# Moving columns in short runs: the value products of a hybrid encoder layer read and write in another order

## The chip, the cores and the metric

The kernel runs on one core of a Trainium2 chip. A core has a matmul engine (TensorE, "PE" in the profile, its weight loads "PEld"), VectorE (DVE), ScalarE (ACT), GpSimd (POOL) and SyncE (SP), which issues most of the transfers. Operands lie in on-chip memory of 128 partitions; products add up in another memory of 128 partitions, whose banks hold 512 numbers of four bytes per partition. The metric is the device time of one execution in microseconds, the median of several runs, lower is better.

## The reference

One layer of an encoder trunk on 256 tokens of width 2048, all in fp32: a norm, one wide projection, an attention branch with latent vectors, a state-space branch run forward and backward, two gates, an output projection, and a gated feed-forward block with a short convolution. The change lies in the attention branch, in the values `v`:

```python
kv = (rms_norm(kv_lat, kv_norm_w) @ w_ukv).reshape(bsz, s_len, MLA_HEADS, QK_NOPE_DIM + V_HEAD_DIM)
k_nope, v = kv[..., :QK_NOPE_DIM], kv[..., QK_NOPE_DIM:]
...
p = jax.nn.softmax(sc.astype(jnp.float32) * scale, axis=-1).astype(v.dtype)
return jnp.einsum("bhqk,bkhd->bqhd", p, v)
```

`kv_lat` has 512 channels, `v` has 16 heads of 128 channels, so the values are a product of 256 x 512 by 512 x 2048.

## The kernel before

All products are made from two halves of each fp32 number. A value is rounded to the matmul engine's fp32r format (the high part) and the rest is kept (the low part); a product is then three: high by high, high by low, low by high. For a matmul, the stationary operand (`lhsT`, 128 x 128) is loaded first, and the moving operand (`rhs`, 128 partitions by up to 512 columns) streams past it; each of its columns adds into the column of the sums that stands at the same place in the output's order.

The work is a list of *jobs*. A job loads one slab of weights (128 partitions x 16 blocks of 128 columns) into one of three `raw` buffers, splits it in two halves of 8 blocks (`split_to`: ScalarE makes `wh` at L215, VectorE makes `wl` at L216, five buffers of each), and runs its products. Splits run up to five halves ahead of the products and loads up to three slabs ahead. Evacuations and small work ("sides") are attached to places in the list. The opening of the kernel is put in order by hand; after it, a planner orders the instructions of each engine by their place in the list and its own costs, with waits where buffers or results are needed.

The list of this stage has gate jobs (`g`: L277 to L279), rope jobs (`R`), value jobs (`V`) and query-key jobs (`QK`: L221 to L223), written out by hand at L1495:

```python
for it in "g R0 g g g V0 QK0 g QK1 g V1 QK2 g QK3 V2 R1 g QK4 g QK5 g V3 QK6 g QK7 g g g g g".split():
```

A value job (`v_job`, one for each group of four heads) has the latent tokens as its stationary operand (`hi` and `lo`, four blocks of 128 channels by 256 tokens) and the slab as its moving one. A half of the slab holds two blocks of channels, each with 512 value columns side by side. For each half `h`, token block `t` and channel block `kk` it makes three products of 512 columns (L663, L664, L665) into a bank of sums; the two token blocks have a bank each. So a job has 2 x 2 x 2 x 3 = 24 products, and the four jobs have 96. At the end, ScalarE copies the sums' high part (L670) and VectorE takes the rest (L671); attention multiplies them later (`att3`, L221 to L223 with `vh` and `vl`).

Elsewhere in the kernel, the dense products (L242) have a moving operand of two runs of 256 columns, the high and the low part of a page of tokens, and write 512 contiguous sums; L249 follows them with 256 contiguous columns.

Of the kernel before, what the change touches and what calls it, by code (L numbers as in the profile page):

```python
# [65 lines left out]
def tile_bidir_hybrid_layer(ctx: ExitStack, tc, xT, pos, vec, cst, w_in, w_r, w_v, w_qk, w_oa,  # L66
# [9 lines left out]
    act, dve, pe = nc.scalar, nc.vector, nc.tensor  # L76

    def page(shape, dt=F32, name="pg"):
        return pp.tile(shape, dt, tag="pg", bufs=NPG, name=name)
# [4 lines left out]
    def gpsum(shape):  # L84
        return gps.tile(shape, F32, tag="g", name="g")
# [4 lines left out]
    def f32(ap):  # L90
        return ap.bitcast(F32)
# [523 lines left out]
    def r_job(i):  # L615
# [30 lines left out]
        jobs.append(j)  # L646
        return j, ro

    def v_job(i):
        hi, lo = lat["kvHL"]  # L650
        cell = {}

        def mm(h, n, wh, wl):
            if h == 0:
                cell["ps"] = [gpsum([P, 512]), gpsum([P, 512])]
            wH = wh.rearrange("p (k b) m -> p k (b m)", k=2)
            wL = wl.rearrange("p (k b) m -> p k (b m)", k=2)
            for t in range(2):
                ts = slice(t * P, (t + 1) * P)
                for kk in range(2):  # L660
                    k = 2 * h + kk
                    ps = cell["ps"][t]
                    pe.matmul(ps, lhsT=hi[:, k, ts], rhs=wH[:, kk, :], start=k == 0, stop=False)  # L663
                    pe.matmul(ps, lhsT=hi[:, k, ts], rhs=wL[:, kk, :], start=False, stop=False)  # L664
                    pe.matmul(ps, lhsT=lo[:, k, ts], rhs=wH[:, kk, :], start=False, stop=k == 3)  # L665

        def ev():
            vh, vl = page([P, 2, 512], F32R, name="vh"), page([P, 2, 512], F32R, name="vl")
            for t in range(2):
                act.activation(vh[:, t, :], cell["ps"][t], AF.Copy)  # L670
                dve.tensor_sub(vl[:, t, :], cell["ps"][t], f32(vh[:, t, :]))  # L671
            vv[i] = (vh, vl)
        j = Job(w_v[i], 16, mm, ev)
        jobs.append(j)
        return j
# [808 lines left out]
    def Vj(i):  # L1484
        defer(v_job, w_v, i)
# [28 lines left out]
    for g in range(G):  # L1514
        b = len(jobs)
# [22 lines left out]
    b = len(jobs)  # L1538
# [23 lines left out]
    b = len(jobs)  # L1562
# [12 lines left out]
    b = len(jobs)  # L1575
# [134 lines left out]
    while i < len(jobs):  # L1710
# [3 lines left out]
        if j.whole:  # L1714
            ps = j.whole()
# [106 lines left out]
```

## Time and profile before

| | us |
|---|---|
| median of 3 runs | 1931.13 (1930.81 to 1931.7) |
| profiled execution | 1931.8 |
| its span | 1930.0 |
| TensorE busy | 1918.2 |
| VectorE busy | 1609.9 |
| ScalarE busy | 1284.1 |
| first and last start of a value product (L663) | 94.5 and 213.1 |

The profile is of one execution. Its span runs from the first to the last instruction; the execution's time has 1.8 us more around it. A row of a group gives line, engine, operation, output and inputs, shapes and count, then busy time, mean length of one in ns, and the idle time before. A matmul's length includes the time that its last columns take to come out, so lengths of successive matmuls overlap, and the pace is read from their starts in the timeline.

### The profile page before, as it was taken

The numbers are of one execution on the slowest core, as the hardware profiler recorded it, in microseconds if no ns is written. First come the engines' busy times: TensorE is split into PE (matmuls) and PEld (weight loads), VectorE is DVE, ScalarE is ACT, GpSimd is POOL, SyncE is SP. The second block draws the span as 40 slices with busy tenths as digits, with TensorE's granted clock in tenths as the row PEclk, the third lists the DMA queues.
The fourth block names the chain that finished last, engine by engine and source line by source line (L and its number), as shares of the span: only waits on it lengthen the run. The fifth ranks groups of instructions, "written<-read, shape, count | busy, mean of one in ns | idle before, by whom it ended". The sixth has DMA issues, their size and how long they took to land.

```text
span 1930.0 us, 28942 instructions
## 1 busy us (share of the span) xinstructions
PE 1918.2 (99%) x10834; PEld 1675.3 (87%) x10834; DVE 1609.9 (83%) x2628; ACT 1284.1 (67%) x2038; POOL 17.3 (1%) x38
## 2 busy tenths in 40 slices
PE   9999999999999999999999999999999999999998
PEld 8899988888888888888888888888888888888887
DVE  7887779979779779779898886898989889898675
ACT  6566555878887888878665555776656566655564
POOL 0200000000000000000000000000000000000000
PEclk9999999999999999999999999999999999999999
DMA  8644447765665565564566675567766666668983
GB/s 298 197 166 142 162 134 233 269 228 168 216 233 170 209 239 169 204 240 164 173 197 201 214 270 200 202 224 227 250 238 230 215 221 224 217 219 326 312 308 118
DMA packets 180525, 416.15 MB, mean 216 GB/s; under 512 B 11392, under 2 KB 114496, under 8 KB 152480
## 3 DMA queue, kind: packets, MB, share of 16 engines
q1 hardware_dynamic: 178816, 412.06, 63.3%
q0 software_dynamic: 1088, 1.67, 0.3%
q8 instruction: 85, 1.39, 0.3%
q10 hardware_dynamic: 480, 0.57, 0.1%
q14 instruction: 56, 0.46, 0.1%
HBM read 398.29 MB, written 13.34 MB: 213 GB/s over the span
## 4 chain that ended last, share of the span: by engine, by line
PE 92%; DVE 3%; DMA 2%; ACT 1%; issue 0%; SPq 0%; DVEq 0%; ACTq 0%
PE g L242 37%; PE g L249 19%; PE g L985 9%; PE s L1178 5%; PE g L277 3%; PE g L278 3%; PE g L279 3%; PE s L985 2%; DVE wl L216 1%; PE g L221 1%; DMA raw<-in_w_os 1%; PE g L223 1%; PE g L222 1%; PE s L242 1%; PE s L890 1%; PE s L899 1%
## 5 line engine op out<-in xcount | busy, mean ns | idle before, releaser
L216 DVE TENSOR_TENSOR wl<-raw,wh 128x1024 fp32r<-128x1024 f32 x621 | 745.6, 1214 | 183.2 <-ACT wh L215 104.6
L215 ACT ACTIVATE wh<-raw 128x1024 fp32r<-128x1024 f32 x621 | 641.4, 1049 | 274.9 <-PE g L242 89.6
L242 PE MATMUL g<-xHL,wh 128*128 128x512 f32 x1408 | 337.7, 392 | 0.3 <-DVE cu L292 0.3
L242 PE MATMUL g<-hHL,wh 128*128 128x512 f32 x1408 | 327.4, 390 | 0.0
L242 PEld LDWEIGHTS g<-hHL,wh 128*128 128x128 f32 x1408 | 262.6, 188 | 53.8 <-ACT wh L215 0.3
L242 PEld LDWEIGHTS g<-xHL,wh 128*128 128x128 f32 x1408 | 259.6, 188 | 52.0 <-PE s L223 0.4
L249 PEld LDWEIGHTS g<-xHL,wl 128*128 128x128 f32 x1408 | 180.5, 191 | 6.8
L249 PE MATMUL g<-xHL,wl 128*128 128x256 f32 x1408 | 182.6, 283 | 0.0
L249 PEld LDWEIGHTS g<-hHL,wl 128*128 128x128 f32 x1408 | 174.8, 192 | 3.4
L249 PE MATMUL g<-hHL,wl 128*128 128x256 f32 x1408 | 176.0, 283 | 0.0
L985 PE MATMUL g<-wh,yHL 128*128 128x512 f32 x392 | 124.9, 390 | 0.0
L152 ACT ACTIVATE wh<-T 128x1024 fp32r<-128x1024 f32 x60 | 63.6, 1061 | 58.6 <-DVE T L191 22.9
L277 PE MATMUL g<-wh,xHL 128*128 128x512 f32 x256 | 100.4, 392 | 0.0
L278 PE MATMUL g<-wl,xHL 128*128 128x512 f32 x256 | 100.0, 390 | 0.0
L279 PE MATMUL g<-wh,xHL 128*128 128x512 f32 x256 | 99.8, 390 | 0.0
L1123 DVE SCALAR_TENSOR_TENSOR uc<-u,V,uc 128x255 f32<-128x255 f32 x176 | 84.5, 480 | 15.3 <-ACT uc L1121 14.1
L153 DVE TENSOR_TENSOR wl<-T,wh 128x1024 fp32r<-128x1024 f32 x60 | 73.4, 1223 | 16.4 <-ACT wh L152 14.1
L985 PEld LDWEIGHTS g<-wh,yHL 128*128 128x128 f32 x392 | 73.6, 188 | 15.2
L242 PE MATMUL g<-aHL,wh 128*128 128x512 f32 x336 | 79.8, 390 | 0.0
L985 PE MATMUL g<-wl,yHL 128*128 128x512 f32 x196 | 76.5, 390 | 0.9 <-DVE wl L216 0.9
L1121 ACT ACTIVATE uc<-u,V 128x256 f32<-128x256 f32 x88 | 52.3, 595 | 34.4 <-DVE u L292 31.1
L242 PEld LDWEIGHTS g<-aHL,wh 128*128 128x128 f32 x336 | 62.6, 188 | 12.7
(413 smaller groups left out, 3078.1 us busy)
## 6 DMA issues: line engine op xcount, KB each, us to landing
raw<-in_w_in SPq DMA_DIRECT2D x88, 1024.0 KB, 4.8
raw<-in_w_up SPq DMA_DIRECT2D x88, 1024.0 KB, 4.8
raw<-in_w_in SPq DMA_DIRECT2D x128, 256.0 KB, 4.0
raw<-in_w_os SPq DMA_DIRECT2D x32, 1024.0 KB, 6.2
raw<-in_w_dn SPq DMA_DIRECT2D x44, 512.0 KB, 4.7
raw<-in_w_dn SPq DMA_DIRECT2D x66, 256.0 KB, 4.9
raw<-in_w_oa SPq DMA_DIRECT2D x16, 1024.0 KB, 5.7
FB<-acsD SPq DMA_DIRECT2D x32, 512.0 KB, 7.3
```

What stands on the lines that cost most here:

```text
L152: act.activation(wh, v, AF.Copy)
L153: dve.tensor_sub(wl, v, f32(wh))
L215: act.activation(vh, r, AF.Copy)
L216: dve.tensor_sub(vl, r, f32(vh))
L242: pe.matmul(ps, lhsT=wh[:, b, :], rhs=x, start=k == 0, stop=False)
L249: pe.matmul(cell["ps"][:, 0, :], lhsT=wl[:, b, :], rhs=get(k)[:, 0, :], start=False, stop=k == ktot - 1)
L277: pe.matmul(ps, lhsT=x[:, 0, ts], rhs=wH[:, kk, :], start=k == 0, stop=False)
L278: pe.matmul(ps, lhsT=x[:, 0, ts], rhs=wL[:, kk, :], start=False, stop=False)
L279: pe.matmul(ps, lhsT=x[:, 1, ts], rhs=wH[:, kk, :], start=False, stop=k == kt - 1)
L985: pe.matmul(M[nm], lhsT=x, rhs=w, start=left[nm] == total[nm], stop=left[nm] == 1)
L1123: dve.scalar_tensor_tensor(o[:, a], u[:, b], vcol("fcw", k * 88 + cb), o[:, a], ALU.mult, ALU.add)
L1178: pe.matmul(M[nm], lhsT=x, rhs=w, start=left[nm] == 3 * NK, stop=left[nm] == 1)
```

## The change

The products at L663 and L664 walk their moving columns and their sums in another order. A view of 512 columns is seen as four places of 128 columns. With `w = 16` the walk takes 16 columns of the first place, 16 of the second, of the third and of the fourth, then the next 16 of the first, and so on; with `w = 2` it takes two of each in turn. The high-by-high product goes in runs of 16, the high-by-low product in runs of 2; the low-by-high product (L665 before) keeps its contiguous order. The moving operand and the sums are viewed in the same way, so each column still adds into the same sum. Stationary operands, loads, splits and evacuations are the same.

```diff
+    def in_runs(ap, w):
+        return ap.rearrange("p (b m w) -> p m b w", b=4, w=w)
+
     def v_job(i):
...
-                    pe.matmul(ps, lhsT=hi[:, k, ts], rhs=wH[:, kk, :], start=k == 0, stop=False)
-                    pe.matmul(ps, lhsT=hi[:, k, ts], rhs=wL[:, kk, :], start=False, stop=False)
+                    pe.matmul(in_runs(ps, 16), lhsT=hi[:, k, ts], rhs=in_runs(wH[:, kk, :], 16), start=k == 0,
+                              stop=False)
+                    pe.matmul(in_runs(ps, 2), lhsT=hi[:, k, ts], rhs=in_runs(wL[:, kk, :], 2), start=False,
+                              stop=False)
                     pe.matmul(ps, lhsT=lo[:, k, ts], rhs=wH[:, kk, :], start=False, stop=k == 3)
```

## The prediction

> **What bounds the kernel now.** I read the totals of the page and the clock line first, then the chain that ended last, then the waits of TensorE from the first value job to the end.
>
> ```profile
> span 1930.0 us, 28942 instructions
> PE 1918.2 (99%) x10834; PEld 1675.3 (87%) x10834; DVE 1609.9 (83%) x2628; ACT 1284.1 (67%) x2038; POOL 17.3 (1%) x38
> PEclk9999999999999999999999999999999999999999
> PE 92%; DVE 3%; DMA 2%; ACT 1%; issue 0%; SPq 0%; DVEq 0%; ACTq 0%
> ...
> PE g L985 <- DVE wl L216: 0.9, 2, 0.5
> PE s L1276 <- ACT m L1256: 0.7, 1, 0.7
> PE g L242 <- DVE cu L292: 0.3, 1, 0.3
> PE s L1178 <- DVE wl L153: 0.2, 1, 0.2
> ```
>
> The matmul engine is busy for 99% of the span at full granted clock and makes up 92% of the chain. From 94 us on (the first value job starts at 94.53) it waits for 0.9 + 0.7 + 0.3 + 0.2 = 2.1 us in all. So a product that holds the array longer moves the end by nearly the same amount: at most 2.1 us can be swallowed by later waits. Busy time alone wouldn't prove this, because a matmul's record includes its drain; that is why the starts are read next.
>
> The three lines of the value job, and the first and last rows of the first job (V0) and the last (V3), from the timeline (start, length, instruction):
>
> ```profile
> L663 PE MATMUL g<-wh,latH 128*128 128x512 f32 x32 | 12.6, 393 | 0.0
> L664 PE MATMUL g<-wl,latH 128*128 128x512 f32 x32 | 12.5, 391 | 0.0
> L665 PE MATMUL g<-wh,latL 128*128 128x512 f32 x32 | 12.5, 390 | 0.0
> L664 PEld LDWEIGHTS g<-wl,latH 128*128 128x128 f32 x32 | 6.0, 188 | 1.1
> ...
> 94.53 0.39 PE L663 MATMUL g<-wh,latH 128*128 128x512 f32 x1
> 94.76 0.39 PE L664 MATMUL g<-wl,latH 128*128 128x512 f32 x1
> ...
> 99.75 0.39 PE L665 MATMUL g<-wh,latL 128*128 128x512 f32 x1
> 99.97 0.28 PE L221 MATMUL g<-latH,wh 128*128 128x256 f32 x1
> ...
> 208.32 0.40 PE L663 MATMUL g<-wh,latH 128*128 128x512 f32 x1
> ...
> 213.56 0.39 PE L665 MATMUL g<-wh,latL 128*128 128x512 f32 x1
> 213.79 0.28 PE L221 MATMUL s<-pT,vh 128*128 128x256 f32 x1
> ```
>
> V0 has 24 products between 94.53 and 99.97: 5.44 / 24 = 226.7 ns from start to start. V3 has 24 in 213.79 - 208.32 = 5.47, or 227.9 ns. The 390 ns in the group rows is the length of one product with its drain; the pace is 227 ns, and the pace is what counts. A weight load takes 188 ns, inside that pace. No row shows an idle gap before any of the 96 products. All four jobs together hold the array for 96 x 0.227 = 21.8 us, 1.1% of the span. The two changed lines are 64 of these products, 14.5 us.
>
> **How much of the pace is columns.** Products of 256 columns run beside products of 512:
>
> ```profile
> 396.92 3.79 PE L242 MATMUL g<-xHL,wh 128*128 128x512 f32 x16
> 400.55 2.08 PE L249 MATMUL g<-xHL,wl 128*128 128x256 f32 x16
> 402.46 3.82 PE L242 MATMUL g<-xHL,wh 128*128 128x512 f32 x16
> ```
>
> The sixteen of 256 columns take 402.46 - 400.55 = 1.91 us, 119.4 ns each. Against 226.7 ns for 512, a column costs (226.7 - 119.4) / 256 = 0.419 ns, so 512 columns cost 214.6 ns and 12.1 ns are fixed.
>
> **The change, part by part.** Nothing is added or removed: the same 10834 matmuls, the same weight loads (the stationary operand is untouched), the same loads from memory, the same waits. Both operands that take the new order take the same one, so that column 5 of the slab still adds into column 5 of the sums. What changes is the walk. With runs of 16 (L663), a product reads 32 runs and jumps 31 times. With runs of 2 (L664), it reads 256 runs and jumps 255 times. Each jump goes 128 columns, or 512 bytes, further along, and after the fourth place back. Reads of the slab and writes of the sums make it together.
>
> *The jump itself.* The trace of before has no product with runs this short. The nearest rows are those of L242: its moving operand is two runs of 256 columns (the high and the low part of a token page), one jump per product, while its sums lie contiguous. Sixteen of them take 400.55 - 396.92 = 3.63 us, 226.9 ns each, against 226.7 ns for the contiguous V0. A jump on the read side therefore costs 0.2 ns, with a resolution of some 0.9 ns (0.01 us on each sum, over 16 and 24 products). The bound below is nothing. The bound above is 0.2 + 0.9 = 1.1 ns a jump; there are 32 x (31 + 255) = 9152 jumps, 10.1 us. I take nothing, since the rows of one jump and none agree to 0.2 ns, and keep both ends.
>
> *A read or write that uses only part of what it fetches.* This isn't priced by the jump of L242, whose runs are long. If pairs are too short for the array's rate, the plainest price is half rate, one more 214.6 ns per product: 32 x 0.2146 = 6.87 us for the pairs alone, 13.7 us if runs of 16 suffer as well. I take nothing here too, nearest to the row that has any jump at all.
>
> The Trainium skill speaks on both sides. Advanced Engine Details and Errata (SBUF Cachelines) has lines of 16 bytes and asks for two hits in a line to keep full performance: a pair of fp32 is exactly two. Its next section (PSUM Cachelines) has lines of 8 bytes and asks that every two consecutive elements be contiguous, which a pair meets, and yet says that any non-contiguous access pattern slows matmuls significantly. By the first two statements the sum stays at +0; by the last all 64 products lose, and the rival "both kinds" below is what that would be here. No run here has yet shown any of it.
>
> *Adding to a sum written shortly before.* With one order throughout, a column of the sums is written again 512 columns later. With the orders in turn the distance shrinks: column 127 is the 506th of the order in pairs and the 128th of the contiguous product behind it, so 134 columns or 56 ns lie between. From an L665 to an L663 on the same bank (16 of the 32; the others follow on the other bank) the least is 176 columns. The rows of L249 show sums written again after 256 columns at the full pace (119.4 ns), and no row shows less. Bound below: nothing. Bound above, if 256 columns were needed: (256 - 134) x 0.419 = 51 ns for each of 32 L665, and (256 - 176) x 0.419 = 34 ns for 16 of the L663, 1.6 + 0.5 = 2.1 us. I take nothing; even the whole of it would lie within what can be told from no change.
>
> *Covers.* The edit is costed at nothing because the columns stream at the same rate, not because something hides it; there is no cover, as the waits show. If a product grew, what is late next is in the waits and the groups around these jobs (85 to 240 us):
>
> ```profile
> ACT vh L670 <- PE g L665: 2.1, 4, 0.8
> ACT wh L215 <- PE g L279: 17.2, 11, 2.5
> ...
> L670 ACT ACTIVATE vh<-g 128x512 fp32r<-128x512 f32 x8 | 4.7, 597 | 2.1 <-PE g L665 2.1
> ```
>
> ScalarE reads the finished sums (L670), and it already waits for them and for free slab buffers (L215, 17.2 us in these rows); it would wait a bit longer and then be no later relative to TensorE, since it and VectorE are ahead here. They gain room.
>
> *A gain.* A product can't stream fewer than its 512 columns; if all of the fixed 12.1 ns vanished from 64 products, that would be 0.8 us. Together with every later wait (2.1) it is 2.9 us, under 0.2%.
>
> The sum: the profiled execution took 1931.8 us, its span 1930.0 and 1.8 around it; plus 0 it stays 1931.8. That execution lies 0.7 above the median of the three runs, 1931.13 (1930.81 to 1931.7). The forecast is stated against that median: **1931.1 us, no change**. A measurement of this kernel tells about 0.2%, 3.9 us, from no change.
>
> **The rivals.**
>
> *Pairs at half rate (the other side: slower).* One mechanism: in L664, reading or writing pairs from four places fetches more than it uses, so that the 512 columns take twice as long; runs of 16 are long enough. +6.87 us, 1938.0. It decides as soon as a pair costs more than 3.9 / 32 = 122 ns extra per product, 57% above its columns' time. For it: no product before has runs under 128 columns, so nothing shows that pairs stream. Against it: a jump alone is free to 0.2 ns.
>
> *A fixed price per jump.* One column (0.419 ns) lost at each of 9152 jumps: 3.83 us, 1935.0, right at the bound. The L242 rows allow it (1.1 ns) but point lower.
>
> *Both kinds at half rate.* 13.7 us, 1944.9. It would need runs of 16, 64 bytes long, to be as bad as pairs; against it stands the same L242 row, though for reads only.
>
> *Dearer pairs.* A quarter of the rate, 3 x 214.6 x 32 = 20.6 us, 1951.7; nothing in the trace speaks for it.
>
> *The walk isn't what changes.* If the order of instructions moves (from the 94.53 us of V0 on, a planner fills in the work of several jobs), the time goes by that alone: down by at most the 2.1 us of waits, or up by a wait that appears. Or the new walk is turned back to a straight one when the program is built, which can't be told from the forecast by the time, only by equal records of L663 to L665.
>
> **How the numbers follow.** No price (or only the short distance): 0.64. Pairs at half rate: 0.15. A price per jump: 0.07, of which I count 0.04 within the bound. Both kinds: 0.07. Dearer pairs: 0.03. Another order: 0.04, half of it a gain, a quarter each no change and a loss. Slower is 0.15 + 0.03 + 0.07 + 0.03 + 0.01 = 0.29; within 0.2% is 0.64 + 0.04 + 0.01 = 0.69; faster is 0.02. The forecast's own range is 1929.9 to 1933.2: the lowest run less the runs' spread of 0.9, and the median plus the 2.1 us of the short distance. The range for 8 in 10 goes to pairs at half rate with the runs' scatter above their median: 1931.13 + 6.87 + 0.6 = 1938.6. Beyond it lie both kinds and the dearer pairs, 0.10.
>
> **What the changed profile would show.** Right: starts of L663, L664 and L665 still 227 ns apart, a value job still 5.44 to 5.47 us, records near 390 ns. Pairs at half rate: 441 ns from each L664 to the L665 behind it and a job of 5.44 + 8 x 0.215 = 7.16 us. A price per jump of one column: 240 ns behind L663 and 334 ns behind L664. Both kinds: 441 ns behind each. The short distance: a gap before L665, with L664 itself unchanged. Another order: other lines between those of a value job, or new rows among the waits of TensorE. The forecast is wrong if the value jobs take over 1 us longer each.

## The result and the profile after

The changed kernel takes 1937.19 us (median of 5 runs, 1936.68 to 1938.33) against 1930.81 us before (5 runs, 1929.26 to 1931.7). The ratio is 1.0034, with a 95% interval of 1.0023 to 1.0045: it is slower by 6.4 us, between 4.4 and 8.7.

The page of the changed kernel, and the waits of TensorE behind the value jobs (from 222 us on):

```profile
span 1936.0 us, 28943 instructions
PE 1925.7 (99%) x10834; PEld 1676.6 (87%) x10834; DVE 1610.9 (83%) x2628; ACT 1284.5 (66%) x2038; POOL 17.2 (1%) x38
...
PE s L1281 <- ACT m L1261: 0.7, 1, 0.7
PE s L1183 <- DVE wl L153: 0.3, 1, 0.3
PE g L242 <- DVE cu L292: 0.2, 1, 0.2
```

The number of matmuls is the same, and TensorE is busy for 7.5 us longer. The other engines are as before. The groups of the value jobs, by line (L666 reads in runs of 16, L668 in pairs, L670 contiguous):

```profile
L668 PE MATMUL g<-wl,latH 128*128 128x512 f32 x32 | 20.2, 631 | 0.0
L670 PE MATMUL g<-wh,latL 128*128 128x512 f32 x32 | 13.5, 421 | 0.0
L666 PE MATMUL g<-wh,latH 128*128 128x512 f32 x32 | 12.5, 392 | 0.0
```

Before, all three were 390 to 393 ns long. Now the pairs are 631, and the contiguous product behind them 421, while the runs of 16 are as they were. The timeline of V0 (start, length, instruction):

```profile
94.61 0.39 PE L666 MATMUL g<-wh,latH 128*128 128x512 f32 x1
94.84 0.63 PE L668 MATMUL g<-wl,latH 128*128 128x512 f32 x1
95.28 0.42 PE L670 MATMUL g<-wh,latL 128*128 128x512 f32 x1
95.54 0.39 PE L666 MATMUL g<-wh,latH 128*128 128x512 f32 x1
...
102.03 0.28 PE L221 MATMUL g<-latH,wh 128*128 128x256 f32 x1
```

V0 lasts 102.03 - 94.61 = 7.42 us, against 5.44 before. Averaged over its eight rounds, the steps are 230 ns from the runs of 16 to the pairs, 440 ns from the pairs to the contiguous product, and 258 ns from there to the next round. The other jobs last 7.42, 7.43 and 7.42. All four are 29.69 us; before they were 5.44, 5.47, 5.77 and 5.47, or 22.15 us (the third had two longer steps, of 310 and 410 ns, which are gone). TensorE thus loses 7.54 us here. The span grew by 6.0 us. Of the difference, 0.9 us is a wait that went: TensorE waited 2.1 us behind the value jobs before and waits 0.7 + 0.3 + 0.2 = 1.2 us now. L985 no longer waits for a split of its slab, probably because the splits had more time. For the remaining 0.6 us no row accounts; runs of one kernel differ by some 2 us among themselves, so it may be scatter.

The 30 ns on L670 come together with a longer weight load. Two loads before the change, then the loads of V0 after it and their group:

```profile
94.54 0.19 PEld L664 LDWEIGHTS g<-wl,latH 128*128 128x128 f32 x1
94.76 0.19 PEld L665 LDWEIGHTS g<-wh,latL 128*128 128x128 f32 x1
```

```profile
94.85 0.19 PEld L670 LDWEIGHTS g<-wh,latL 128*128 128x128 f32 x1
95.30 0.21 PEld L666 LDWEIGHTS g<-wh,latH 128*128 128x128 f32 x1 [0.26 <-issue]
95.55 0.19 PEld L668 LDWEIGHTS g<-wl,latH 128*128 128x128 f32 x1
...
L666 PEld LDWEIGHTS g<-wh,latH 128*128 128x128 f32 x32 | 6.6, 205 | 7.4 <-issue 7.4
```

Before and after, a load starts 10 to 20 ns behind the start of the product ahead of its own. So the load for L670 is done early in the slow product. The next one, for L666, starts at 95.30, as L670 has just started; it isn't later than others in that, but it takes 205 ns on average in place of 188. Which of the two holds the other up, the product or the load, these rows don't show.

### The profile page after: what moved, and what is told of

Read it like the earlier page. It is cut to its first block, busy times and chain, and to the rows that moved or that the text cites. A ratio compares the mean times of both kernels' runs of the same rounds, so it can differ in the third digit from the quotient of the medians.

```text
span 1936.0 us, 28943 instructions
## 1 busy us (share of the span) xinstructions
PE 1925.7 (99%) x10834; PEld 1676.6 (87%) x10834; DVE 1610.9 (83%) x2628; ACT 1284.5 (66%) x2038; POOL 17.2 (1%) x38
## 4 chain that ended last, share of the span: by engine, by line
PE 94%; DVE 3%; ACT 1%; DMA 1%; issue 0%; SPq 0%; DVEq 0%; ACTq 0%
PE g L242 37%; PE g L249 19%; PE g L990 11%; PE s L1183 5%; PE g L277 3%; PE g L278 3%; PE g L279 3%; PE s L990 2%; PE g L221 1%; PE g L223 1%; PE g L222 1%; DVE wl L216 1%; PE g L668 1%; PE s L242 1%; PE s L895 1%; PE s L904 1%
## 5 line engine op out<-in xcount | busy, mean ns | idle before, releaser
L242 PE MATMUL g<-xHL,wh 128*128 128x512 f32 x1408 | 337.7, 392 | 0.2 <-DVE cu L292 0.2
L242 PE MATMUL g<-hHL,wh 128*128 128x512 f32 x1408 | 327.4, 390 | 0.0
L242 PEld LDWEIGHTS g<-hHL,wh 128*128 128x128 f32 x1408 | 262.6, 188 | 53.8 <-ACT wh L215 0.3
L242 PEld LDWEIGHTS g<-xHL,wh 128*128 128x128 f32 x1408 | 259.6, 188 | 52.0 <-PE s L223 0.4
L242 PE MATMUL g<-aHL,wh 128*128 128x512 f32 x336 | 79.8, 390 | 0.0
L242 PEld LDWEIGHTS g<-aHL,wh 128*128 128x128 f32 x336 | 62.6, 188 | 12.7
```

The lines of the kernel that those rows point to most:

```text
L242: pe.matmul(ps, lhsT=wh[:, b, :], rhs=x, start=k == 0, stop=False)
```

## The experiments

In all of them, the *step* is the time from the start of a product to the start of the next, averaged over the eight products of that line in a value job. Contiguous products take 227 ns. The kernels under "How the step depends on the walk" ran once each; of them only steps are used, not times.

### Which product, and reading or writing

Four kernels on one chip, beside a median of 1930.55 us for the kernel before (21 runs).

The runs of 16 alone:

```diff
-pe.matmul(in_runs(ps, 2), lhsT=hi[:, k, ts], rhs=in_runs(wL[:, kk, :], 2), start=False, stop=False)
+pe.matmul(ps, lhsT=hi[:, k, ts], rhs=wL[:, kk, :], start=False, stop=False)
```

> Only the high-by-high product keeps its runs of 16; the high-by-low product is contiguous again. Theory 'pairs alone lose': the starts stay 227 ns apart, the job at 5.44 us, the time within 0.2% of before (1930.8). Theory 'every run loses something': 32 products at runs of 16 would show a pace above 227 ns; a price per jump of one column gives 240 ns behind each and +0.4 us in all.

Measured: 1931.31 us, ratio 1.0004 (0.9995 to 1.0012), no change. V0, from its first product to the one behind it:

```profile
96.11 0.39 PE L666 MATMUL g<-wh,latH 128*128 128x512 f32 x1
...
101.66 0.28 PE L221 MATMUL g<-latH,wh 128*128 128x256 f32 x1
```

That is 5.55 us, 0.11 more than before; the steps are 229 to 233 ns. Runs of 16 cost next to nothing: 22.49 us in the four jobs against 22.15. That sum is near the 0.4 us of the price per jump, but this theory had 240 ns behind each L666, where 229 are measured.

The pairs alone:

```diff
-pe.matmul(in_runs(ps, 16), lhsT=hi[:, k, ts], rhs=in_runs(wH[:, kk, :], 16), start=k == 0, stop=False)
+pe.matmul(ps, lhsT=hi[:, k, ts], rhs=wH[:, kk, :], start=k == 0, stop=False)
```

> Only the high-by-low product keeps its pairs. Theory 'pairs alone lose': 441 ns behind each pair product as in the changed kernel, and the whole of its loss, +6.4 us over before. If the 30 ns behind the low-by-high product come from the pairs, they stay (256 ns to the next product); if they come from the runs of 16 that follow it, they go and the pace there is 227 ns, the loss then 5.5 us.

Measured: 1939.83 us, ratio 1.0049 (1.0036 to 1.0061). The pairs carry the whole loss, and a bit more of it than the changed kernel has. Three starts in V0:

```profile
95.50 0.67 PE L667 MATMUL g<-wl,latH 128*128 128x512 f32 x1
95.99 0.41 PE L669 MATMUL g<-wh,latL 128*128 128x512 f32 x1
96.24 0.39 PE L666 MATMUL g<-wh,latH 128*128 128x512 f32 x1
```

The step behind the pairs is 440 to 520 ns here, 478 on average: it goes 460, 490, 520, 440 and begins again. The extra on the product behind them stays (255 ns): it doesn't come from the runs of 16. The four jobs last 30.81 us, 8.66 more than before.

Then reading and writing apart:

```diff
# read_pairs
+pe.matmul(ps, lhsT=hi[:, k, ts], rhs=in_runs(wL[:, kk, :], 2), start=False, stop=False)
# write_pairs
+pe.matmul(in_runs(ps, 2), lhsT=hi[:, k, ts], rhs=wL[:, kk, :], start=False, stop=False)
```

> The high-by-low product reads its moving columns in pairs from four places, but writes its sums in their contiguous order, so those columns add into other sums than in the reference; the amount of work is the same. Theory 'the read is slow': 441 ns behind each of these products and the time of the changed kernel, about +6.4 us. Theory 'the write is slow': 227 ns and the time of before.

> The reverse: the high-by-low product reads its moving columns in contiguous order and writes its sums in pairs to four places, so those columns add into other sums than in the reference. Theory 'the read is slow': 227 ns and the time of before. Theory 'the write is slow': 441 ns, about +6.4 us. If both this and the read alone cost the same, either alone is enough and the two overlap.

Measured: reading 1938.23 us, ratio 1.0040 (1.0027 to 1.0054); writing 1931.03 us, ratio 1.0005 (0.9996 to 1.0014). The groups of the kernel that only reads in pairs, then of the one that only writes in pairs:

```profile
L667 PE MATMUL g<-wl,latH 128*128 128x512 f32 x32 | 21.2, 664 | 0.0
L668 PE MATMUL g<-wh,latL 128*128 128x512 f32 x32 | 13.3, 416 | 0.0
```

```profile
L667 PE MATMUL g<-wl,latH 128*128 128x512 f32 x32 | 12.5, 391 | 0.0
L668 PE MATMUL g<-wh,latL 128*128 128x512 f32 x32 | 12.5, 390 | 0.0
```

With the read alone the records and the four jobs (30.82 us) are those of the pairs on both sides. With the write alone the jobs last 5.44, 5.47, 5.77 and 5.47 us, to the hundredth what they were before. The loss is in reading the moving operand, and there it is in the pairs. The step is the same in all four jobs (479, 479, 480 and 479 ns with the read alone), so walks may be compared across jobs.

### How the step depends on the walk

Only the high-by-low product is changed in the next ones, on the read side, with another walk in each value job. A walk is given by its places and its run; the places are 2048 bytes divided by their number apart.

```diff
+WALKS = [(4, 1), (4, 4), (4, 8), (4, 2)]          # places, run, by job
+pe.matmul(ps, lhsT=hi[:, k, ts], rhs=walk(wL[:, kk, :], *WALKS[i]), start=False, stop=False)
```

> Only the high-by-low product reads otherwise, from four places in turn, and writes contiguous, so its columns add into other sums than in the reference. Run length by value job: V0 1, V1 4, V2 8, V3 2. Theory F (each fetch brings 16 bytes, four columns, and takes the time of four columns, whether they are used or not): from this product to the next 227 + 3 x 214.6 = 871 ns in V0, 227 in V1 and V2, 441 in V3 (some 30 ns more behind a contiguous product). Theory J (a jump costs two columns, 0.84 ns): 656 ns in V0, 333 in V1, 280 in V2, 441 in V3. Theory L (two columns of a 16-byte line are enough): it gives 227 in V3 and falls already.

Measured: 271, 261, 235 and 479 ns. Rows of V0 (singles) and V3 (pairs):

```profile
95.61 0.43 PE L669 MATMUL g<-wl,latH 128*128 128x512 f32 x1
95.88 0.39 PE L670 MATMUL g<-wh,latL 128*128 128x512 f32 x1
...
214.83 0.67 PE L669 MATMUL g<-wl,latH 128*128 128x512 f32 x1
215.32 0.41 PE L670 MATMUL g<-wh,latL 128*128 128x512 f32 x1
```

Theories F and J fall on the singles, which jump most and cost only 44 ns more than a contiguous product (F had 871 ns, J 656). Theory L falls on the pairs. Fours and eights are near the contiguous pace, as theory F had it, and not as a price per jump.

```diff
+RUN = [1, 2, 4, 8]
+    v = wl.rearrange("p b c -> p (b c)").rearrange("p (g s) -> p g s", s=2 * n)
+    return v[:, :, :n]
```

> Only the high-by-low product reads otherwise: always forward through the 1024 columns of a half slab, taking n and leaving out n: n is 1 in V0, 2 in V1, 4 in V2, 8 in V3. So it multiplies other columns of the slab than the reference does, as many of them, and writes contiguous. Nothing jumps far or back. Theory F: 441 ns in V0 and V1 (half of each 16 bytes used), 227 in V2 and V3 (all used, every second fetch left out). Theory J: 656, 441, 333, 280. Theory D (only far jumps cost): 227 in all four.

Measured: 440, 434, 233 and 233 ns. Rows of V0 (one of two) and V2 (four of eight):

```profile
95.49 0.61 PE L670 MATMUL g<-wl,latH 128*128 128x512 f32 x1
95.93 0.41 PE L671 MATMUL g<-wh,latL 128*128 128x512 f32 x1
...
160.96 0.40 PE L670 MATMUL g<-wl,latH 128*128 128x512 f32 x1
161.19 0.39 PE L671 MATMUL g<-wh,latL 128*128 128x512 f32 x1
```

This is theory F's table to within 10 ns, and theories J and D miss it. Nothing jumps far, and yet half of each 16 bytes used is half rate, so distance isn't what makes pairs slow; whole groups of 16 bytes with gaps between them run at the full pace.

> Only the high-by-low product reads otherwise: pairs in all four jobs, but from 2, 8, 32 and 128 places in turn (V0 to V3), which are 1024, 256, 64 and 16 bytes apart; it writes contiguous, so its columns add into other sums than in the reference. Theory F and theory J: 441 to 475 ns in all four. Theory D (distance): falling towards 227 ns in V2 and V3. A theory that four places 512 bytes apart collide in the memory: 441 only where the places are 256 bytes or more apart, or other numbers in V0 and V1 than in the changed kernel.

Measured (2, 8, 32, 128 places): 326, 529, 416 and 438 ns. Rows of V0 and of V1:

```profile
96.25 0.51 PE L669 MATMUL g<-wl,latH 128*128 128x512 f32 x1
96.58 0.41 PE L670 MATMUL g<-wh,latL 128*128 128x512 f32 x1
...
129.73 0.73 PE L669 MATMUL g<-wl,latH 128*128 128x512 f32 x1
130.26 0.43 PE L670 MATMUL g<-wh,latL 128*128 128x512 f32 x1
```

Near places don't help (438 ns at 16 bytes apart), so theory D is out. But eight places cost 90 ns more than half rate and two places cost 115 less: something is added to the half rate, and something is saved.

```diff
+P2, P16 = (4, 2), (4, 16)
+IN = [(P2, P2, P2), (P16, P2, P16), (P2, None, None), (None, None, None)]
+OUT = IN[:3] + [(None, (128, 2), None)]
```

> Output as the reference. V0: all three products in pairs on both sides. V1: runs of 16, pairs, runs of 16. V2: only the high-by-high product in pairs. V3: all reads contiguous, the high-by-low product writes pairs to 128 places 8 bytes by 8 bytes, 16 bytes apart. The changed kernel has 441 ns from the pairs to the next product and 256 from that to the one behind it; with a contiguous product ahead of the pairs it was some 475. Theory 'the 30 ns belong to the change of order from pairs to contiguous': V0 441 throughout, V1 256 or less behind the pairs' follower, V2 the same extra behind the pairs' follower. Theory 'they belong to the weight load that is late behind a slow product': the same 30 ns in V1 and V2 as before, and in V0 a pace near 441 as each load is early. V3: 227 ns if writing pairs is free at any distance.

Measured, steps behind the first, second and third product: V0 453, 440 and 440 ns; V1 231, 476, 254; V2 479, 254, 229; V3 228, 231, 224. Three rows of V0:

```profile
96.04 0.62 PE L670 MATMUL g<-wh,latH 128*128 128x512 f32 x1
96.49 0.62 PE L671 MATMUL g<-wl,latH 128*128 128x512 f32 x1
96.93 0.62 PE L672 MATMUL g<-wh,latL 128*128 128x512 f32 x1
```

Among themselves, pairs take 440 ns with no extra behind them, save some 10 ns in the first of the three. The product behind a slow one pays some 25 ns whether it is contiguous (V2) or in runs of 16 (V1). The two theories had nearly the same numbers here, so this doesn't part them. Other jobs bear on it: behind the singles from four places, which change the order as much and take only 271 ns, the contiguous product takes 230 ns; it takes 246 behind the pairs from two places (326 ns) and 266 behind those from eight (529 ns). So the extra comes with a slow product and not with a change of order as such; that the longer weight load makes it isn't shown. Writes to places 16 bytes apart are free as well (V3). That a pair product takes 440 ns in some company and 479 in other isn't explained by any of this.

> Only the high-by-low product reads otherwise, single columns from 2, 8, 32 and 128 places in turn (V0 to V3), and writes contiguous, so its columns add into other sums than in the reference. Singles from 4 places took 271 ns, where theory F (every fetch of 16 bytes costs four columns) had 871: F alone has fallen. Theory R (a fetched 16 bytes stay at hand for about four columns, so what is read again within that costs nothing): about 227 ns from 2 places, and 871 from 8, 32 and 128, where each column comes back to its 16 bytes after 8 or more. Theory N (number of runs doesn't matter, only pairs are bad): near 271 ns throughout.

Measured (2, 8, 32, 128 places): 216, 528, 414 and 443 ns. Rows of V0 and V1:

```profile
95.88 0.38 PE L669 MATMUL g<-wl,latH 128*128 128x512 f32 x1
96.10 0.39 PE L670 MATMUL g<-wh,latL 128*128 128x512 f32 x1
...
130.29 0.73 PE L669 MATMUL g<-wl,latH 128*128 128x512 f32 x1
130.82 0.43 PE L670 MATMUL g<-wh,latL 128*128 128x512 f32 x1
```

From 8 places on, singles cost what pairs do, within 5 ns. Theory R falls with its 871: one column used of 16 bytes isn't quarter rate but half, as two are. Its other half holds: from 2 places a single is free, and even 11 ns faster than contiguous.

> As before, but runs of four columns, 16 bytes each, from 2, 8, 32 and 64 places in turn (V0 to V3). Theory R: every fetch is used whole, 227 ns throughout, up to the 261 that four places showed. A theory by which far jumps cost of themselves: more from 2 places (1024 bytes apart) than from 64 (32 bytes apart).

Measured (2, 8, 32, 64 places): 249, 274, 228 and 229 ns. Rows of V1, the dearest:

```profile
130.34 0.44 PE L669 MATMUL g<-wl,latH 128*128 128x512 f32 x1
130.61 0.39 PE L670 MATMUL g<-wh,latL 128*128 128x512 f32 x1
```

Runs of 16 bytes are at the full pace from 32 and 64 places and lose 22 to 47 ns where the places are 256 to 1024 bytes apart, most at 256, as the pairs and singles do. Theory R allowed up to 261, so the 274 miss it; distance alone doesn't order them either, as 256 bytes cost more than 1024.

```diff
+WALKS = [(4, 2, 496), (4, 2, 480), (8, 2, 480), (4, 4, 480)]      # places, run, columns
```

> Pairs from four places 496 bytes apart (V0, 496 columns in place of 512), 480 bytes apart (V1, 480 columns), from eight places 240 bytes apart (V2, 480 columns), and fours from four places 480 bytes apart (V3, 480 columns); the high-by-low product leaves out the last 16 or 32 columns and adds into other sums than the reference. Theory 'places a power of two apart collide': pairs fall to half rate without more, 12 + 2 x 0.419 x 496 = 428 ns and 414 ns, eight places from 529 to 414, fours from 261 to 213. Theory 'no collision, only use of the fetch': V0 and V1 the 441 to 479 of the powers of two, less 3 and 6%, V2 some 495, V3 245.

Measured: 419, 406, 419 and 221 ns. Rows of V2 and V3:

```profile
161.68 0.60 PE L669 MATMUL g<-wl,latH 128*128 128x480 f32 x1
162.09 0.41 PE L670 MATMUL g<-wh,latL 128*128 128x512 f32 x1
...
214.81 0.38 PE L669 MATMUL g<-wl,latH 128*128 128x480 f32 x1
215.03 0.39 PE L670 MATMUL g<-wh,latL 128*128 128x512 f32 x1
```

The collision theory had 428, 414, 414 and 213; without it 428 to 465, 415 to 450, 495 and 245 were due. V2 and V3 decide: eight places 240 bytes apart take 419 ns where 256 took 529, and fours 480 bytes apart take 221 where 512 took 261. The columns left out (480 in place of 512) would save only 34 and 16 ns of that by the theory without collision. So the extra at 256 and 512 bytes is gone at nearby distances that are no power of two. Why it arises isn't shown ("collide" is the theory's word), and two places, 1024 bytes apart, weren't tried off the power of two. All walks together (ns, 512 columns; forward reads n and skips n; run 16 is the high-by-high product, which also writes in runs):

| run | 2 places | 4 | 8 | 32 | 64 | 128 | forward |
|---|---|---|---|---|---|---|---|
| 1 | 216 | 271 | 528 | 414 | | 443 | 440 |
| 2 | 326 | 440 to 479 | 529 | 416 | | 438 | 434 |
| 4 | 249 | 261 | 274 | 228 | 229 | | 233 |
| 8 | | 235 | | | | | 233 |
| 16 | | 230 | | | | | |

### A faster version

The 216 ns of singles from two places were tried where many products can use it. The sums come out interleaved, and the copies put them back in order:

```diff
+TWO = (2, 1)
-pe.matmul(ps, lhsT=x[:, 0, ts], rhs=wH[:, kk, :], start=k == 0, stop=False)
+pe.matmul(ps, lhsT=x[:, 0, ts], rhs=walk(wH[:, kk, :], TWO), start=k == 0, stop=False)
... (all three products of gate and value jobs)
-act.activation(store[q][:, t, :], ps, AF.Tanh, scale=0.5)
+act.activation(plain(store[q][:, t, :], TWO), back(ps, TWO), AF.Tanh, scale=0.5)
```

> A trial of a gain, made from the kernel before. Single columns from two places 1024 bytes apart took 216 ns from their product to the next, against 227 contiguous. Here all three products of the 32 gate jobs (768 products) and of V0 read so, and write contiguous; the sums then stand interleaved, and ScalarE (and VectorE for the values) put them in order as they copy them out. V1 to V3 read all three products in fours from 32 and 64 places and eights from 16, put in order in the same way. The output is the reference's. Theory 'the 11 ns are friction of contiguous reading that this walk avoids': 216 ns in the gates, 768 x 11 = 8.4 us and 1 us in the value jobs, about 0.45% faster. Theory 'the 11 ns came from the neighbours' (a product is short only between others, or the start of the next moves): 227 ns in a row of like products and the time of before. Slower only if the copies out of order hold the sums too long.

Measured: 1924.21 us (1923.53 to 1924.85, 5 runs) beside 1930.81 for the kernel before, ratio 0.9966 (0.9952 to 0.9980): 0.34% faster, 6.6 us. The first value job, a gate group, and ScalarE's copy of the sums:

```profile
93.57 0.38 PE L675 MATMUL g<-wh,latH 128*128 128x512 f32 x1
...
98.75 0.28 PE L221 MATMUL g<-latH,wh 128*128 128x256 f32 x1
...
L289 PE MATMUL g<-wl,xHL 128*128 128x512 f32 x256 | 97.0, 379 | 0.0
...
L682 ACT ACTIVATE vh<-g 128x512 fp32r<-128x512 f32 x8 | 4.7, 596 | 1.9 <-PE g L677 1.8
```

24 products in 98.75 - 93.57 = 5.18 us are 215.8 ns each: the short step is the product's own, not its neighbours'. The gate products are 379 ns long in place of 390, and the 36 ahead of V0 stand 215.8 ns apart as well. ScalarE's copies take 596 ns as before (597), though they now read every second column in V0 and runs of four and eight in V1 to V3. V1 and V3, in fours and eights, took 5.43 and 5.31 us, between contiguous and V0; V2, in fours, took 5.80, no less than before (5.77). The 9.4 us expected were 6.6, with an interval of 3.9 to 9.3. Two shares of the gap are in the profile: the value jobs gave 0.4 us (21.72 in all) where 1 was due, and TensorE's waits from 94 us on grew from 2.1 to 3.4 us.

## Why the prediction was wrong

- **What bounds the kernel** held. A longer product moves the end by most of its length: 7.54 us more on TensorE, 6.0 us more in the span of the profiled execution and 6.4 in the medians. The prediction let at most 2.1 us be swallowed by later waits; 0.9 were. Its 21.8 us for the four jobs came from V0 and V3 alone; with the longer steps of V2 they took 22.15.
- **The failing step** is "A read or write that uses only part of what it fetches", and there the choice: "I take nothing here too, nearest to the row that has any jump at all". The row of L242 bounded a jump between long runs, and did that rightly: runs of 16 cost 0.3 us in all jobs, or 0.3 ns for each of 992 jumps. It said nothing of runs shorter than 16 bytes, and was taken for a row that did. The term was put at +0; the pair products measured some 213 ns more each, 6.8 us for the 32. The prediction had named that gap itself ("This isn't priced by the jump of L242") and should have weighed the two ends evenly.
- **What stood in its place** is the rival "pairs at half rate": 441 ns behind each L668 and 1938.0 us; measured 440 ns and 1937.19 us. Its job of 7.16 us was 7.42, because the product behind each pair pays 30 ns more, which no part had. That its time came out so close is partly luck: the jobs lost 7.54 us and not 6.87, and the end moved by less than that. The other part of its wording, "reading or writing", is settled: reading.
- **A price per jump** had 240 and 334 ns; measured 230 and 440, and fours with 127 jumps at 228 to 229 ns, so no. **Both kinds at half rate**: the runs of 16 are free. **Another order**: the rows of the value jobs stand in the same sequence.
- **Sums written shortly before** cost nothing: the kernel that only writes in pairs has the 134 columns and the same four job lengths to the hundredth. The extra before L666 isn't this, since it is there in pairs read alone.
- **A gain** was said to be bounded by the 12.1 ns beyond the columns, and by 0.8 us in these jobs. The walk from two places takes 11 of the 12.1 ns. So "fixed" was the wrong word, and the bound was right.
- **The rules weighed.** The Trainium skill, Advanced Engine Details and Errata (SBUF Cachelines), asks for two hits in a line of 16 bytes. The trace disagrees for fp32 moving operands: two of four columns run at half rate (438 ns from 128 places, 434 forward), just as one of four does (443 ns from 128 places). Near the full pace are whole groups of four (228 to 274 ns) and singles from two or four places (216 and 271), whose 16 bytes come back within two to four columns; pairs from two places, which come back as soon, take 326. The Trainium skill says in the next section of that page (PSUM Cachelines) that any non-contiguous access pattern slows matmuls significantly. The runs disagree for the sums: writing in pairs gave 226 to 231 ns and no change in time at 512 bytes from place to place, and 228 ns at 16 bytes.

What stays open: why pairs from four places take 440 or 479 ns by their neighbours (with places 496 and 480 bytes apart the same neighbours gave 419 and 406, with no such cycle); why one column and two of each 16 bytes cost the same; whether the savings at two and four places are bytes that are still at hand (singles from 2 and 4 places and pairs from 2 come back to them within four columns, all others later, which fits, but nothing shows the mechanism). Runs of four that begin inside a group of 16 bytes were not tried, nor single columns on the side of the sums.

## What to carry to other kernels

Let the moving columns of an fp32 matmul come in runs of at least 16 bytes: pairs and singles took 326 to 529 ns here where contiguous columns took 227, except singles in turn from two or four places, and most of that lands on the span where TensorE is the bound. If the order has to change, change it on the side of the sums, where pairs and runs of 16 cost nothing. For short runs, keep places off distances of 256 and 512 bytes; two places 1024 bytes apart cost fours 22 ns, and made singles faster. And a row that bounds one resource (a jump) doesn't bound another that it never stressed (how much of a fetch is used): give such an unknown both ends by weight.

## What the runs showed that was not expected

Contiguous reading isn't the fastest walk: single columns in turn from two places 1024 bytes apart gave 215.8 ns per product of 512 against 226.7, in 768 gate products, together with the value jobs, 6.6 us of the whole kernel. A copy out of the sums at every second column took the same 596 ns as a contiguous one. And the cost of a walk doesn't fall evenly with its run: from four places singles took 271 ns, pairs 440 to 479, fours 261.
